# Which engine makes the low parts of the weights, and what the emission plan counts

## Chip, cores and metric

One core of a Trainium2 chip. The metric is the device time of one execution in microseconds. The profile's names of the engines are PE (TensorE's matmuls), PEld (its weight loads), DVE (VectorE), ACT (ScalarE), POOL (GpSimd) and SP (SyncE, which here issues the DMAs).

## What is computed

Two layers of a decoder trunk over 256 tokens of width 1024, all in float32:

```
for l in range(DEPTH):                       # DEPTH = 2
    h = rms_norm(x, attn_norm[l])
    x = x + hybrid_mixer(h, ..., w_in[l], ..., w_out[l])
    h = rms_norm(x, ffn_norm[l])
    x = x + conv_ffn(h, w_up[l], conv_w[l], conv_b[l], w_down[l])
```

`hybrid_mixer` multiplies h with one wide matrix `w_in`, makes three attention branches of the columns (MoBA block attention; NSA with a compressed, a selected and a window part; GLA, a gated linear attention that needs the logarithm of a sigmoid and a cumulative sum), and merges them by gates. `conv_ffn` multiplies with `w_up`, runs a causal convolution of width 3 over one half of the columns, a GELU, a product with the other half, and multiplies with `w_down`.

## The kernel before

**Weights in two parts.** Every weight matrix streams from HBM in blocks of 128 partitions by up to 1024 columns (`raw`, 5 buffers). A block is split into a high part (`whi`, a cast to float32r on ScalarE) and a low part (`wlo` = `raw` - `whi`, a subtraction), 3 buffers each. The activations are split in the same way (`hh`, `hl`; `fh`, `fl` in the feed-forward part). Each product is three matmuls: high by high, high by low, low by high. Chunks of mode A have activations as the stationary operand and up to 512 weight columns moving; chunks of mode B (the up projection and some columns of the input projection) have weights stationary and 256 tokens moving. A block of a mode B chunk is used by 24 matmuls, and a chunk of it has two blocks.

**Who makes the low part.** `Pump.split` emits one ScalarE cast for a block, and then divides the low part's columns between VectorE and GpSimd. The division comes from the plan's times of the two engines: columns go to GpSimd until both would end together. `lo(a, b)` emits VectorE's subtraction, `lo(a, b, G)` GpSimd's. The first two blocks of the kernel are handled apart, in `first`; the second one's low part stands on GpSimd.

**The emission plan.** The program is straight-line code, and each engine runs its instructions in the order in which they were emitted. That order is chosen while the program is built. `Plan` keeps a modelled time for each engine (`t`) and for each piece of a tile (`at`). Every emitted instruction passes through `Eng`, whose line 135 is the line that nearly all rows of the profile carry; `Plan.note` takes its start as the latest of its engine's time, TensorE's time and its inputs' times plus 0.15 us, and adds `Plan.cost`. The main loop (`run_phase`) emits the matmuls of block after block. Everything else (the attention branches, the epilogues) is written as generators; a generator that yields is resumed by `tick` when TensorE's modelled time has passed the modelled end of its last step plus 0.8 us. So a modelled cost sets no time on the chip, but it sets how many matmuls TensorE has in its queue ahead of a small step, and in which order VectorE, ScalarE and GpSimd find their work. `run_phase` holds a block back in the plan until its high part is there, not its low part.

**Places that the text speaks of.** `nsa_keys` normalises keys (`kn`), transposes them on TensorE into PSUM (`pst`) and scales them into `kt` by four VectorE operations, which TensorE then reads for the scores. `compress` copies `kd` for another transposition. `gla_gate` adds a bias, takes Exp and Ln on ScalarE behind a load of their activation table, and on VectorE subtracts (`tt<-tt`) and scans into `b`, which `gla` reads. In the up projection a pair of chunks makes two tiles of columns: `done_a` scales by the norm (`tt<-pd,rsB`), convolves (four `tt<-tt,pt`), applies the GELU on ScalarE and scales again on GpSimd (`tt<-tt,rsB`); `done_g` multiplies with the other half (`tt<-tt,pd`), casts to `fh` on VectorE and makes `fl` on GpSimd. There are 11 pairs in a layer. Tiles `tt` are 9 scratch buffers.

Of the kernel before, what the change touches and what calls it, by code (L numbers as in the profile page):

```python
# [27 lines left out]
def _aps(args, kw):  # L28
    outs, ins = [], []
    for i, a in enumerate(args):  # L30
        if hasattr(a, "tensor"):
            (outs if i == 0 else ins).append(a)
    for k, a in kw.items():
        if hasattr(a, "tensor"):
            (outs if k in ("out", "accum_out") else ins).append(a)
    return outs, ins


def _free(ap):
    n = 1  # L40
    for d in ap.shape[1:]:
        n *= d
    return n
# [4 lines left out]
    return lo, lo + 1 + sum(abs(s) * (n - 1) for s, n in ap.ap[1:])  # L48


class Plan:


    def __init__(self):
        self.t = {"PE": 0.0, "V": 0.0, "A": 0.0, "G": 1.5, "S": 0.6, "D": 0.0}
        self.at = {}
        self.step = 0.0
        self.n = 0
# [14 lines left out]
    def cost(self, e, f, outs, ins, kw):  # L73
        n = max(_free(a) for a in outs[:1] + ins[:1]) if outs else 0
        if e == "PE":
            m = _free(outs[0])
            if f == "transpose":
                return 0.109
            if ins[0].dtype == F32R:
                return max(0.107, m / 2400 + 0.0025)  # L80
            return max(_free(ins[0]) / 600, m / 600 + 0.004)
        if e == "V":
            if f == "reciprocal":
                return 0.07 + n * 0.0084
            if f == "tensor_tensor_scan":
                return 0.07 + n * 0.00104
            if f == "memset":
                return 0.05 + n * 0.0003
            fast = f in ("tensor_scalar", "tensor_copy") and "pst" not in str(ins[0].tensor) and "pd" not in str(ins[0].tensor)
            ptr = len(ins) > {"tensor_scalar": 1, "scalar_tensor_tensor": 2}.get(f, 9)  # L90
            return 0.07 + 0.06 * ptr + n * (0.00052 if fast else 0.00104)
        if e == "S":
            return 0.06
        if e == "A":
            if f == "dma_start":
                return 0.06
            return 0.11 + n * 0.00083 + 0.05 * ("pst" in str(ins[0].tensor) or "pd" in str(ins[0].tensor)) + 0.09 * (len(outs) - 1 + hasattr(kw.get("bias"), "tensor"))
        if f == "dma_start":
            return 1.0
        if f in ("memset", "iota"):  # L100
            return 0.1 + n * 0.0009
        if kw.get("op") == OP.pow:
            return 0.35 + 0.165 * n
        return 0.1 + n * (0.0036 if f == "tensor_copy" else 0.0023)

    def note(self, e, f, args, kw):
        outs, ins = _aps(args, kw)
        if not outs:
            return
        self.n += 1  # L110
        st = max([self.t[e], self.t["PE"]] + [self.get(a) + 0.15 for a in ins])
        if f == "dma_start":
            self.t[e] = st + self.cost(e, f, outs, ins, kw)
            self.t["D"] = max(self.t["D"], self.t[e] + 1.0) + 4 * _free(outs[0]) * outs[0].shape[0] / 360e3
            en = self.t["D"] + 1.5
        else:
            en = st + self.cost(e, f, outs, ins, kw)
            self.t[e] = en
        lat = 0.2 if e == "PE" else 0.0
        for a in outs:  # L120
            self.put(a, en + lat)
        if f != "dma_start":
            self.step = max(self.step, en + lat + 0.15)
# [29 lines left out]
def trunk_kernel(ctx, tc, x, rel_bias, attn_norm, w_in, moba_q_norm, moba_k_norm,  # L153
# [13 lines left out]
    pd = ctx.enter_context(tc.tile_pool(name="pd", bufs=4, space=PSUM))  # L167
# [7 lines left out]
    def take(s, n=1):  # L175
        while True:
            t = s.at(n)
            if t is not None and t <= plan.t["PE"]:
                break
            plan.step = max(plan.step, t or 0.0)  # L180
            yield
        s.take(n)

    def give(s, n=1):
        s.free += [plan.step] * n
# [4 lines left out]
    def pst():  # L190
        return ps.tile([128, 512], F32, name="pst", tag="pst")

    def tt():
        return tp.tile([128, 512], F32, name="tt", tag="tt", bufs=NT)

    plan = Plan()
    V, A, G, PE, SP = (Eng(plan, e, g) for e, g in (("V", nc.vector), ("A", nc.scalar), ("G", nc.gpsimd),
                                                    ("PE", nc.tensor), ("S", nc.sync)))

    def avail(*aps):  # L200
        while max(plan.get(a) for a in aps) > plan.t["PE"]:
            plan.step = max([plan.step] + [plan.get(a) for a in aps])
            yield
# [14 lines left out]
    class Pump:  # L218
# [43 lines left out]
        def split(self):  # L262
            n, hi, lo = self.open()
            hi(0, n)
            w = self.blocks[self.ns - 1][1]
            h = self.hl[self.ns - 1][0]
            t0 = plan.get(h)
            v, g = max(plan.t["V"], t0) + 0.07, max(plan.t["G"], t0) + 0.1 + 0.0
            c = n * w
            m = int((v - g + c * 0.00104) / (0.00104 + 0.0023)) // 64 * 64  # L270
            m = c if m > c - 128 else m if m >= 128 else 0
            if m < c:
                lo(0, c - m)
            if m:
                lo(c - m, c, G)

        def ahead(self, d, s):
            while self.nd < min(len(self.blocks), self.ng + d):
# [65 lines left out]
    def wait(*fl):  # L344
        for f in fl:
            while f not in flags:
                yield
# [290 lines left out]
    def make_layer(l):  # L638
        key = lambda *a: (l,) + a
        st = {}  # L640
        T = {}

        def atl(name, shape, dt=F32, **kw):
            t = at.tile(shape, dt, name=name, tag=name, **kw)
            T[name] = t
            return t
# [9 lines left out]
        def setf(f):  # L656
            flags.add(key(f))
# [22 lines left out]
        def gla_gate():  # L680
            ga = T["ga"]
            yield from avail(ga)
            yield from take(sem_ps)
            p = pst()
            for t in range(2):
                PE.transpose(p[:16, t * 128:t * 128 + 128], ga[:, t], ident)
            yield from take(sem_t)
            gg = tt()
            gw, gl = gg[:16, 0:256], gg[:16, 256:512]
            SP.dma_start(gw, gla_gate_w[l])  # L690
            yield
            V.tensor_copy(gl, p[:16, :256])
            give(sem_ps)
            yield
            yield from wait(("par", l))
            yield from avail(gw)
            yield from take(sem_ps)
            p = pst().rearrange("p (c s) -> p c s", c=2)
            for c in range(2):
                PE.matmul(p[:, c], gw[:, c * 128:c * 128 + 128], gl, start=True, stop=True)  # L700
            give(sem_t)
            yield
            yield from take(sem_t, 2)
            u, m = tt(), tt()
            pt = par[l][0]
            for c in range(2):
                A.activation(u[:, c * 256:c * 256 + 256], p[:, c], AF.Abs, bias=pt[:, 22 + c:23 + c])
                V.tensor_scalar(m[:, c * 256:c * 256 + 256], p[:, c], pt[:, 22 + c:23 + c], 0.0,
                                op0=OP.add, op1=OP.min)
            give(sem_ps)  # L710
            A.preload_act_table_set("natural_log_exp_and_others")
            A.activation(u, u, AF.Exp, scale=-1.0)
            A.activation(u, u, AF.Ln, bias=1.0)
            setf("ln")
            V.tensor_sub(m, m, u)
            b = atl("b", [128, 512])
            V.tensor_tensor_scan(b, smask, m, 0.0, op0=OP.mult, op1=OP.add)
            give(sem_t, 2)
            setf("b")
# [427 lines left out]
        def done_gv(half):  # L1147
            def f(p):
                yield from wait((key("n1"), "rs"))
                gv = grp("gvv", 2048, 1024).rearrange("p (t c) -> p t c", t=2)  # L1150
                T["gvv"] = gv
                if half:
                    ga = atl("ga", [128, 2, 16])
                    for t in range(2):
                        A.activation(ga[:, t], p[t][:, 256:272], AF.Copy, scale=rs(t))
                for t in range(2):
                    A.activation(gv[:, t, half * 256:half * 256 + 256], p[t][:, 0:256], AF.Copy, scale=rs(t))
                give(sem_pd, 2)
                if half:
                    normal.append(gla_gate())  # L1160
                else:
                    setf("gv")
            return f
# [420 lines left out]
    for l, ly in enumerate(layers):  # L1584
        st = ly["st"]
# [64 lines left out]
```

## Time and profile before

| | |
|---|---|
| median of 3 runs | 859.55 us (858.62 to 860.23) |
| the profiled execution, its own time | 859.51 us |
| its span, first to last instruction | 857.7 us |
| instructions | 13958 |
| mean granted TensorE clock | 0.994 |
| DMA | 143.57 MB, mean 167 GB/s |

The span is what the trace shows; about 1.8 us of the execution's own time lie outside it. The layers are alike: the input projection with the attention, the branch and output projections, the up projection (layer 0: from about 244 us; layer 1: from about 662 us) and the down projection.

### The profile page before, as it was taken

Reading aid. Unit: us, or ns where it says so; the run is one execution under the profiler, and the core shown is the slowest. Engines: PE = TensorE matmul, PEld = TensorE weight load, DVE = VectorE, ACT = ScalarE, POOL = GpSimd, SP = SyncE. Lnnn points to the kernel's source line nnn. Section 1 sums busy time; section 2 is a strip of 40 time slices with the busy share of each in tenths; the row PEclk is TensorE's granted clock in tenths of the full one; section 3 lists DMA queues with packets and bytes.
Section 4 is the critical chain, followed back from the end, with each engine's and each line's share of the span. In section 5 each row is a group of like instructions: output and inputs, shape, how many; then the busy total and the mean of one; then the engine's idle time right before and its main releaser. Section 6 shows DMA issues by size and latency. Waiting matters only on the chain.

```text
span 857.7 us, 13958 instructions
## 1 busy us (share of the span) xinstructions
PE 837.8 (98%) x5173; PEld 750.4 (87%) x5173; DVE 576.3 (67%) x880; ACT 431.8 (50%) x666; POOL 470.6 (55%) x341
## 2 busy tenths in 40 slices
PE   7989999999999989999999999999999999999998
PEld 7878888888889989998898898888888999999886
DVE  4665787456757788884446776854595499887642
ACT  5454555554456445453446545464544644454431
POOL 4533654446546665666545347535575476665653
PEclk9998999999999999999999999999999999999999
DMA  6883444445555555556558444445456555556571
GB/s 199 249 255 88 157 121 130 144 128 192 185 162 173 171 174 182 174 167 217 172 174 229 123 146 123 133 130 156 162 182 196 151 159 183 183 163 210 185 218 49
DMA packets 109976, 143.57 MB, mean 167 GB/s; under 512 B 13677, under 2 KB 71380, under 8 KB 109780
## 3 DMA queue, kind: packets, MB, share of 16 engines
q1 hardware_dynamic: 109892, 142.68, 53.7%
q8 instruction: 41, 0.67, 0.3%
q14 instruction: 27, 0.22, 0.1%
q10 hardware_dynamic: 16, 0.00, 0.0%
HBM read 141.60 MB, written 2.63 MB: 168 GB/s over the span
## 4 chain that ended last, share of the span: by engine, by line
PE 80%; DVE 10%; ACT 3%; issue 2%; DMA 2%; POOL 2%; SPq 0%; DVEq 0%; ACTq 0%; POOLq 0%
PE pd L135 70%; PE pst L135 8%; DVE tt L135 5%; DVE wlo L135 4%; DMA raw<-in_w_in_dram 2%; PE po L135 2%; ACT whi L135 1%; ACT tt L135 1%; POOL tt L135 1%; POOL wlo L135 1%; DVE qz L135 1%; POOL mqs L135 0%; DVE kn L135 0%; POOL fl L135 0%; ACT L135 0%
## 5 line engine op out<-in xcount | busy, mean ns | idle before, releaser
L135 POOL TENSOR_TENSOR wlo<-raw,whi 128x256 fp32r<-128x256 f32 (+10 forms) x222 | 317.8, 1435 | 289.2 <-ACT whi L135 275.7
L135 ACT CAST whi<-raw 128x1024 fp32r<-128x1024 f32 (+3 forms) x267 | 271.5, 1021 | 267.2 <-PE pd L135 124.0
L135 DVE TENSOR_TENSOR wlo<-raw,whi 128x768 fp32r<-128x768 f32 (+12 forms) x261 | 268.2, 1035 | 186.7 <-ACT whi L135 183.5
L135 PE MATMUL pd<-hh,wlo 128*128 128x256 f32 x768 | 217.8, 284 | 4.6 <-DVE wlo L135 4.6
L135 PE MATMUL pd<-hh,whi 128*128 128x256 f32 x768 | 218.7, 285 | 0.2
L135 PE MATMUL pd<-hl,whi 128*128 128x256 f32 x768 | 217.5, 283 | 1.1 <-DVE hl L135 1.1
L135 PE MATMUL pd<-whi,hh 128*128 128x512 f32 (+3 forms) x512 | 206.4, 403 | 3.2 <-ACT whi L135 2.2
L135 PE MATMUL pd<-wlo,hh 128*128 128x512 f32 (+3 forms) x512 | 193.6, 378 | 0.2 <-DVE wlo L135 0.2
L135 PE MATMUL pd<-whi,hl 128*128 128x512 f32 (+3 forms) x512 | 193.7, 378 | 0.0
L135 PEld LDWEIGHTS pd<-hh,wlo 128*128 128x128 f32 x768 | 147.3, 192 | 5.6 <-DVE wlo L135 5.6
L135 PEld LDWEIGHTS pd<-hl,whi 128*128 128x128 f32 x768 | 147.3, 192 | 1.8 <-DVE hl L135 1.5
L135 PEld LDWEIGHTS pd<-hh,whi 128*128 128x128 f32 x768 | 147.3, 192 | 0.9 <-ACT hh L135 0.7
L135 PEld LDWEIGHTS pd<-whi,hh 128*128 128x128 f32 x512 | 98.2, 192 | 19.1 <-ACT whi L135 2.4
L135 PEld LDWEIGHTS pd<-whi,hl 128*128 128x128 f32 x512 | 97.8, 191 | 17.4
L135 PEld LDWEIGHTS pd<-wlo,hh 128*128 128x128 f32 x512 | 98.2, 192 | 14.1 <-DVE wlo L135 0.4
L135 DVE SCALAR_TENSOR_TENSOR tt<-tt,pt 128x255 f32<-128x255 f32 x88 | 86.4, 1003 | 1.6
L135 PE MATMUL pd<-whi,fh 128*128 128x512 f32 x176 | 68.7, 390 | 0.0
L135 PE MATMUL pd<-wlo,fh 128*128 128x512 f32 x176 | 68.7, 390 | 0.0
L135 PE MATMUL pd<-whi,fl 128*128 128x512 f32 x176 | 68.5, 389 | 0.0
L135 POOL TENSOR_TENSOR fl<-tt,fh 128x512 fp32r<-128x512 f32 x22 | 41.4, 1882 | 31.3 <-DVE fh L135 31.3
L135 ACT ACTIVATE tt<-tt 128x512 f32<-128x512 f32 (+1 forms) x52 | 26.0, 531 | 32.9 <-DVE tt L135 32.8
L135 ACT ACTIVATE tt<-tt,nm 128x128 f32<-128x128 f32 (+1 forms) x48 | 21.4, 447 | 41.9 <-DVE nm L135 41.9
(210 smaller groups left out, 837.9 us busy)
## 6 DMA issues: line engine op xcount, KB each, us to landing
raw<-in_w_up_dram SPq DMA_DIRECT2D x88, 512.0 KB
raw<-in_w_in_dram SPq DMA_DIRECT2D x84, 512.0 KB
raw<-in_w_down_dram SPq DMA_DIRECT2D x44, 512.0 KB
raw<-in_w_out_dram SPq DMA_DIRECT2D x16, 512.0 KB
raw<-in_w_branch_gla_dram SPq DMA_DIRECT2D x8, 512.0 KB
raw<-in_w_in_dram SPq DMA_DIRECT2D x8, 396.0 KB
raw<-in_w_branch_moba_dram SPq DMA_DIRECT2D x4, 512.0 KB
raw<-in_w_branch_nsa_dram SPq DMA_DIRECT2D x4, 512.0 KB
```

Source lines behind the costliest of these rows:

```text
L135: return g(*args, **kw)
```

## The change

The change edits the plan and its use. In `Plan.cost` it raises prices of matmuls, scans, VectorE operations and accumulating activations. In `Plan.note` it counts 1.3 us for an explicit load of an activation table, and it keeps one time, `port`, for all operations of VectorE and GpSimd that read no PSUM: such an operation is modelled as starting only when the last one of either engine has ended. In `Pump.split` GpSimd gets columns of a low part only when VectorE's modelled time runs past GpSimd's, the port's and the cast's, at least 256 columns; otherwise VectorE makes the whole low part in one instruction. In `gla_gate` a yield stands between the logarithm on ScalarE and VectorE's subtraction and scan.

```diff
+def _psum(ap):
+    return any(n in str(ap.tensor) for n in ("pst", "pd_", "po_"))
...
     def __init__(self):
+        self.port = 0.0
...
             if ins[0].dtype == F32R:
-                return max(0.107, m / 2400 + 0.0025)
-            return max(_free(ins[0]) / 600, m / 600 + 0.004)
+                return max(0.112, m / 2400 + 0.0135)
+            return max(0.112 if _free(ins[0]) < 65 else 0.224, m / 600 + 0.008)
...
             if f == "tensor_tensor_scan":
-                return 0.07 + n * 0.00104
+                return 0.09 + n * 0.0021
...
-            return 0.07 + 0.06 * ptr + n * (0.00052 if fast else 0.00104)
+            return 0.09 + 0.06 * ptr + n * (0.00052 if fast else 0.00109)
...
-            return 0.11 + n * 0.00083 + 0.05 * ("pst" in str(ins[0].tensor) or "pd" in str(ins[0].tensor)) + 0.09 * (len(outs) - 1 + hasattr(kw.get("bias"), "tensor"))
+            return 0.11 + n * 0.00083 + 0.05 * ("pst" in str(ins[0].tensor) or "pd" in str(ins[0].tensor)) + 0.2 * (len(outs) - 1) + 0.09 * hasattr(kw.get("bias"), "tensor")
...
     def note(self, e, f, args, kw):
         outs, ins = _aps(args, kw)
+        if f == "preload_act_table_set":
+            self.t[e] = max(self.t[e], self.t["PE"]) + 1.3
...
         st = max([self.t[e], self.t["PE"]] + [self.get(a) + 0.15 for a in ins])
+        port = e in "VG" and f != "dma_start" and ins and not any(_psum(a) for a in ins)
+        if port:
+            st = max(st, self.port)
...
             self.t[e] = en
+            if port:
+                self.port = en
...
-            t0 = plan.get(h)
-            v, g = max(plan.t["V"], t0) + 0.07, max(plan.t["G"], t0) + 0.1 + 0.0
+            t0 = plan.get(h) + 0.15
             c = n * w
-            m = int((v - g + c * 0.00104) / (0.00104 + 0.0023)) // 64 * 64
-            m = c if m > c - 128 else m if m >= 128 else 0
+            m = int((plan.t["V"] - max(plan.t["G"], plan.port, t0) - 0.1) / 0.0023) // 64 * 64
+            m = min(c, m) if m >= 256 else 0
+            if m:
+                lo(c - m, c, G)
             if m < c:
                 lo(0, c - m)
-            if m:
-                lo(c - m, c, G)
...
             A.activation(u, u, AF.Ln, bias=1.0)
             setf("ln")
+            yield
             V.tensor_sub(m, m, u)
```

## Rows read from the trace of the kernel before

**Rows 1.** The page: busy us (share of the span) and instructions of each engine.
```profile
PE 837.8 (98%) x5173; PEld 750.4 (87%) x5173; DVE 576.3 (67%) x880; ACT 431.8 (50%) x666; POOL 470.6 (55%) x341
```

**Rows 2.** Waits of PE: waiter, releaser, us in total, times, longest.
```profile
PE pd L135 <- DVE wlo L135: 4.8, 6, 2.5
PE pst L135 <- DVE kt L135: 3.0, 1, 3.0
PE pd L135 <- ACT whi L135: 2.2, 1, 2.2
...
PE pst L135 <- DVE kd L135: 0.6, 1, 0.6
```

**Rows 3.** Windows: length, busy us of five engines, PEclk, DMA share, GB/s.
```profile
19.60:22.90 3.30, 3.30 (x12) 3.29 (x12) 3.08 (x9) 0.86 (x1) 3.00 (x4) 0.50 0.63 178
65.20:70.70 5.50, 5.48 (x15) 4.56 (x16) 3.07 (x13) 1.33 (x6) 0.00 (x0) 0.50 0.52 172
303.00:372.00 69.00, 68.39 (x570) 68.39 (x571) 58.77 (x67) 34.86 (x42) 43.56 (x30) 1.00 0.58 183
```

**Rows 4.** Timeline of ACT, layer 0, input projection: start us, us, instruction, count.
```profile
56.88 1.28 ACT L135 ACT_TABLE_LOAD   x1
58.17 1.30 ACT L135 ACTIVATE tt<-tt 128x512 f32<-128x512 f32 x2
```

**Rows 5.** Timeline of DVE there, 59 to 67 us; idle before, releaser in brackets.
```profile
59.50 0.69 DVE L135 TENSOR_TENSOR tt<-tt 128x512 f32<-128x512 f32 x1 [2.12 <-ACT tt L135]
60.23 1.22 DVE L135 TENSOR_TENSOR_SCAN b<-smask,tt 128x512 f32<-128x512 bf16 x1
61.37 3.31 DVE L135 TENSOR_TENSOR wlo<-raw,whi 128x320 fp32r<-128x320 f32 x2
64.60 1.98 DVE L135 TENSOR_SCALAR kt<-pst,pt 64x256 f32<-64x256 f32 x4
```

**Rows 6.** Timeline of POOL in the same stretch.
```profile
60.48 3.38 POOL L135 TENSOR_TENSOR wlo<-raw,whi 128x704 fp32r<-128x704 f32 x2 [7.04 <-ACT whi L135]
```

**Rows 7.** Groups of instructions: count, busy us, mean ns, idle before, releaser.
```profile
L135 POOL TENSOR_TENSOR wlo<-raw,whi 128x256 fp32r<-128x256 f32 (+10 forms) x222 | 317.8, 1435 | 289.2 <-ACT whi L135 275.7
...
L135 DVE TENSOR_TENSOR wlo<-raw,whi 128x768 fp32r<-128x768 f32 x140 | 142.0, 1014 | 164.8 <-ACT whi L135 162.1 <-PE pst L135 2.6
...
L135 DVE SCALAR_TENSOR_TENSOR tt<-tt,pt 128x254 f32<-128x254 f32 x44 | 47.5, 1080 | 1.6
```

**Rows 8.** Timeline of DVE, up projection of layer 0, 298 to 304 us.
```profile
298.78 4.04 DVE L135 SCALAR_TENSOR_TENSOR tt<-tt,pt 128x255 f32<-128x255 f32 x4
302.74 1.61 DVE L135 TENSOR_TENSOR wlo<-raw,whi 128x640 fp32r<-128x640 f32 x2
```

**Rows 9.** Timeline of POOL in the same stretch.
```profile
300.36 2.18 POOL L135 TENSOR_TENSOR wlo<-raw,whi 128x384 fp32r<-128x384 f32 x2
```

**Rows 10.** Timeline of DVE, input projection of layer 1.
```profile
466.71 0.69 DVE L135 TENSOR_TENSOR tt<-tt 128x512 f32<-128x512 f32 x1 [2.12 <-ACT tt L135]
```

**Rows 11.** Timeline of DVE, up projection of layer 0, one operation at 291 us, then one pair.
```profile
291.28 0.48 DVE L135 SCALAR_TENSOR_TENSOR tt<-tt,pt 128x254 f32<-128x254 f32 x1
...
342.18 0.69 DVE L135 TENSOR_TENSOR tt<-tt,pd 128x512 f32<-128x512 f32 x1 [1.88 <-POOL tt L135]
342.91 0.43 DVE L135 CAST fh<-tt 128x512 fp32r<-128x512 f32 x1
343.25 1.22 DVE L135 TENSOR_TENSOR wlo<-raw,whi 128x1024 fp32r<-128x1024 f32 x1
...
350.29 0.68 DVE L135 TENSOR_TENSOR tt<-pd,rsB 128x512 f32<-128x512 f32 x1
...
353.72 0.69 DVE L135 TENSOR_TENSOR tt<-tt,pd 128x512 f32<-128x512 f32 x1 [1.88 <-POOL tt L135]
```

**Rows 12.** Timeline of POOL in that pair.
```profile
340.86 1.29 POOL L135 TENSOR_TENSOR tt<-tt,rsB 128x512 f32<-128x512 f32 x1
```

**Rows 13.** Timeline of POOL: the first reader of `b` in layer 0.
```profile
93.47 1.03 POOL L135 TENSOR_TENSOR tt<-b 128x512 f32<-128x512 f32 x1
```

## Prediction

> **What bounds the kernel now.** I read the busy line of the page first. TensorE is busy 837.8 of 857.7 us, VectorE 576.3, GpSimd 470.6 [rows 1]. No other engine is near the span, so an edit that moves work between VectorE and GpSimd can pay only where TensorE now stands still, or where it runs at half clock. So the second view is TensorE's own waits [rows 2]: six waits for a low part from VectorE, 4.8 us in total with one of 2.5; one of 3.0 for `kt`; 2.2 for a high part from ScalarE; 0.6 for `kd`; the rest is smaller. The third is the granted clock by stretch [rows 3]. Two stretches ran at 0.50, the 1.2 GHz level: 19.6 to 22.9 us, behind the 2.2 us wait, and 65.2 to 70.7 us, behind the 3.0 us wait; TensorE worked through both, so they cost half their length, 1.65 and 2.75 us. Behind the 2.5 us wait the clock stayed at 1.00 (303 to 372 us) [rows 3]. What can be won is therefore 4.8 + 3.0 + 2.2 + 0.6 + 1.65 + 2.75 = 15.0 us, and the question is who makes VectorE late at these places.
>
> **How the two engines share.** At 60.48 us GpSimd takes two low parts that last 3.38 us [rows 6]; VectorE's scan ends at 61.45, and its own two low parts, 320 and 768 columns, then last 3.31 us [rows 5]. A low part of 1024 columns alone takes VectorE 1.22 us [rows 11], so 1088 columns in two instructions should take about 1.4. The missing 1.9 us is the time in which GpSimd worked. The same shows in the groups: a low part on GpSimd takes 1435 ns in the mean, 256 columns most often, where 512 columns on GpSimd alone take 1.29 us [rows 7, 12], so 256 alone would be near 0.65. One engine stands while the other runs when both work on SBUF. An operation of VectorE on PSUM (0.68 and 0.69 us for 512 columns) shows no such stretch [rows 11].
>
> **Low parts on VectorE alone.** GpSimd's share of a full block, given to it at the same time as VectorE's, ends after about 1.4 us [rows 7], its wait included; VectorE alone takes 1.22 [rows 11]. So the low part is complete about 0.2 us earlier, GpSimd loses most of its low parts, and VectorE gains about 256 columns a block (a quarter of 1.22, 0.3 us) but loses the waits for GpSimd. By the new rule GpSimd gets columns only where VectorE's planned queue runs at least 0.69 us past the last planned SBUF operation (0.1 + 256 x 0.0023), that is behind two or more PSUM operations in a row; I expect under 60 low parts on it, and its busy time at some 155 to 210 us: 470.6 less the 317.8 of all 222 low parts, plus at most 60 of about a microsecond [rows 1, 7]. A raw buffer comes free that much earlier too, so SP's next weight load starts no later; the DMA share was 0.58 in the up projection [rows 3].
>
> What does this pay in the up projection? There the stretch 298 to 304 shows it: four `tt<-tt,pt` operations take 4.04 us [rows 8] where one alone takes 0.48 [rows 11], because GpSimd holds 2.18 us of low parts among them [rows 9] and `fl` ahead of those; the next low part starts at 302.74 [rows 8], and TensorE has waited 2.5 us for it. Four at 0.48 would end 2.1 us sooner. Of the 4.8 us in rows 2 I take 4.0 and leave 0.8 for waits that stay; bounds 0 and 4.8. **B = -4.0.**
>
> Is VectorE then fast enough? A pair of chunks is 96 matmuls. Two passes of the same place are 342.18 and 353.72 us, 11.54 us apart [rows 11], 0.120 us a matmul, the new plan's price (the old one was 0.109). VectorE's own work in it: 4 low parts x 1.22 + 0.68 + 4 x 0.48 + 0.69 + 0.43 = 8.60 us; GpSimd's two remaining operations, 2 x 1.29 = 2.58 [rows 11, 12]. If nothing of the two overlapped, 11.18 us: it fits with 0.36 to spare. Before, GpSimd's low parts came on top, and it fitted. Cost 0; without that cover every 0.1 us a pair costs 2.2 us over 22 pairs.
>
> **Plan's prices, table load and the yield.** In layer 0 VectorE stands 2.12 us in front of `tt<-tt` for ScalarE's Exp and Ln [rows 5], behind a table load of 1.28 us [rows 4] that the old plan counts as nothing. Then come a scan of 1.22 us (old price 0.60, new 1.17), and 3.31 us of low parts; only then `kt` at 64.60, and TensorE waits 3.0 us. The edits meet each link: the yield lets other tasks' VectorE work, `kt` too, stand ahead of `tt<-tt` and the scan; the load is counted; the port is counted. Had `kt` (4 in 1.98 us) stood in the hole of 2.12 us, TensorE would not have waited at all; had it only lost GpSimd's 1.9 us, 1.1 us would be left. What the yield makes late is `b`: its first reader starts at 93.47 us [rows 13], 32 us after the scan, so a few us cost nothing; two scratch buffers of nine are held as long. Bounds 0 and 3.0 + 2.75 = 5.75; I take most, since two mechanisms must both fail for the wait to stay whole. **A = -5.0.** In layer 1 the same hole of 2.12 us stands ahead of `kd` [rows 10]; of the 0.6 for `kd` I take 0.5, bounds 0 and 0.6. **C = -0.5.**
>
> A table load: `tt<-tt` on ScalarE starts 1.29 us after the load's start [rows 4], so 1.3 is the price. The Trainium skill, "ScalarE: Activation LUTs", What ACT_TABLE_LOAD costs, counts a drain of about 1.38 us on top, 2.66 us a switch, by which the new price is half of what it should be and the gain 2.7 us smaller over the two layers, near 854.7 (an estimate). The trace does not agree with that drain.
>
> The start is not touched: the 2.2 us wait for ScalarE and the 1.65 us behind it stay, 0. The tail after the last matmul stays, 0.
>
> **What the new order may cost.** Every instruction is placed by the plan, so all of the order moves. A matmul of 256 columns now counts 0.120 instead of 0.109: a delay of 5 us is filled with 42 matmuls and not 46, and the small TensorE steps of the attention stand some 0.5 us earlier per 5 us. VectorE's and ScalarE's prices rise too, which sets them back. New waits the trace cannot show; below, 0 (or a gain: all remaining small waits go, another 1 us); above, one like that for `kt` with its clock, 5.75. I take 2.0, near the 2.2 and 2.5 us waits of rows 2. **E = +2.0.**
>
> Sum: -5.0 - 4.0 - 0.5 + 2.0 = -7.5 us. The profiled execution took 859.51 us (span 857.7 and 1.8 around it), 0.04 from the median of 859.55: **852.0 us**. A measurement of this kernel tells 0.2%, 1.7 us, from no change.
>
> **Rivals.**
> *The wait for `kt` stays.* The plan puts it late again, A = 0: 857.0. For it: the high part that VectorE turns to next comes from the same late ScalarE, whose cast starts only at the end of that table load, Exp and Ln; against it: the 2.12 us hole. 15%.
> *VectorE becomes the bound of the up projection.* If it stands 1.88 us for GpSimd's `tt` as now and the whole 1.29 for `fl`, a pair is 8.60 + 1.88 + 1.29 = 11.77 us against 11.54: 22 x 0.23 = 5.1 us, and B is lost: 852.0 + 4.0 + 5.1 = 861.1, no change that can be told. Against it: `fl` can run beside VectorE's 1.37 us on PSUM, and `tt` mostly has no low part ahead of it any more. 8%.
> *The re-timed order makes new waits (slower).* Place: the input projection of either layer, where `kd`, `kn`, `kt` feed TensorE. The margin that the too fast matmul price gave is gone; if A fails and layer 1 gets a wait of 3.0 us with its 2.75 us of half clock, 852.0 + 5.0 + 5.75 = 862.8. It decides when the new waits, with what A loses, pass 9.5 us in all. For it: the layer 1 hole has the same size and 0.6 us came of it; against: the prices are nearer to the rows at each place I compared. 17%.
> *A table load costs twice its 1.28 us.* VectorE would stand 1.28 us again in each layer: 852.0 + 2.6 = 854.6. Rows 4 speak against it: 2%. The Trainium skill, "ScalarE: Activation LUTs", What ACT_TABLE_LOAD costs, gives about that.
> *All is won and nothing lost:* 859.5 - 5.75 - 4.8 - 0.6 - 1.0 = 847.3, less a few us where the start's wait shortens by chance: 843 to 848, 8%.
> Forecast (848 to 856): 50%.
>
> Range: the forecast with the deep case, both partial ones and the nearer half of the slow one, 845 to 863 us. About 4 in 100 lie below it, 10 above. Faster by over 0.2%: 50 of the forecast, 12 of the 15, 1 of the 8, 1 of the 17, 2 and 8, 0.74. Within 0.2%: 3, 4 and 2 of the three rivals, 0.09. Slower: 3 of the 8 and 14 of the 17, 0.17.
>
> **What would show it.** GpSimd's low parts under 60 and its busy time under 210 us; VectorE's low parts some 315 us in total with the 1024-column ones near 1.22 in the mean; `tt<-tt,pt` well under its mean of 1080 ns [rows 7], near 600; no wait for `wlo` over 1 us in the up projections; clock 1.00 from 62 to 71 us and no wait for `kt` over 1 us; VectorE's 2.12 us hole before `tt<-tt` gone in both layers. Wrong it would be if TensorE's waits in the two input projections sum to more than before, or if the up projection's pairs take over 11.7 us.

## The result, and the profile after

The changed kernel takes **864.87 us** (median of 20 runs, 861.18 to 873.30), the kernel before, measured with it, 859.04 (20 runs, 857.55 to 862.68): a ratio of 1.0087 [1.0065, 1.0109], slower. The forecast was 852.0, and the time lies above its range. The 20 runs fall into two groups of ten, 861.2 to 862.3 us with a mean granted clock of 0.990 to 0.992 and 867.5 to 873.3 with 0.974 to 0.982, and the median lies between them; the profiled execution, 868.38 us with 0.982, is of the second, so stretches of half clock show longer in it than in half of the runs.

The busy line of the page, against [rows 1]: GpSimd lost two thirds of its work, VectorE gained only 12 us.

```profile
PE 845.0 (98%) x5173; PEld 757.6 (87%) x5173; DVE 588.6 (68%) x883; ACT 429.8 (50%) x666; POOL 167.5 (19%) x129
```

The groups of instructions that answer to [rows 7] (count, busy us, mean ns, idle before, releaser):

```profile
L147 DVE TENSOR_TENSOR wlo<-raw,whi 128x1024 fp32r<-128x1024 f32 (+3 forms) x264 | 340.0, 1291 | 202.1 <-ACT whi L147 201.1
L147 DVE SCALAR_TENSOR_TENSOR tt<-tt,pt 128x255 f32<-128x255 f32 x88 | 42.2, 502 | 1.6
L147 POOL TENSOR_TENSOR tt<-tt,rsB 128x512 f32<-128x512 f32 x22 | 40.9, 1859 | 124.0 <-ACT tt L147 124.0
L147 POOL TENSOR_TENSOR wlo<-raw,whi 128x272 fp32r<-128x272 f32 (+4 forms) x10 | 14.2, 1426 | 36.5 <-ACT whi L147 36.5
```

So far it went much as forecast. What didn't is seen in TensorE's waits (waiter, releaser, total us, times, longest), against [rows 2]:

```profile
PE pst L147 <- DVE kn L147: 4.9, 2, 3.2
PE pst L147 <- DVE tt L147: 4.3, 1, 4.3
PE pd L147 <- DVE hl L147: 3.2, 4, 0.9
PE pd L147 <- ACT whi L147: 2.1, 1, 2.1
...
PE pd L147 <- ACT hh L147: 1.0, 1, 1.0
PE pd L147 <- DVE wlo L147: 0.4, 1, 0.4
```

The waits for `wlo` are down from 4.8 us to one of 0.4 at the kernel's start, and the wait for `kt` is gone. In their place TensorE waits 4.9 us for `kn` (once in each layer) and 4.3 for the `tt` of the compress additions, all in the input projections. The windows (length, busy us of five engines, PEclk, DMA share, GB/s) against [rows 3]:

```profile
20.10:23.50 3.40, 3.40 (x13) 3.39 (x12) 3.09 (x15) 0.85 (x1) 0.38 (x1) 0.50 0.52 163
54.20:74.70 20.50, 16.20 (x59) 14.44 (x59) 11.27 (x25) 3.65 (x7) 0.58 (x1) 0.50 0.42 125
303.00:372.00 69.00, 69.00 (x578) 69.00 (x577) 53.26 (x66) 34.24 (x43) 18.57 (x12) 1.00 0.60 183
484.30:491.10 6.80, 6.80 (x27) 6.14 (x26) 3.52 (x9) 0.98 (x2) 0.00 (x0) 0.50 0.27 77
```

The stretch of the up projection that had the 2.5 us wait now begins some 8 us later and runs without one at full clock (the third row: 69.00 of 69.00). But behind the waits of the input projections TensorE works 16.20 and 6.80 us at 1.2 GHz, which costs half of that, 8.1 + 3.4 us; before, one such stretch of 5.5 us cost 2.75 [rows 3].

Who is late shows on VectorE's timeline of layer 0 (start, duration; idle before and releaser in brackets), against [rows 5]:

```profile
48.99 0.42 DVE L147 TENSOR_REDUCE nqs<-tt 128x4 f32<-128x256 f32 x1 [2.81 <-ACT tt L147]
...
50.89 1.23 DVE L147 TENSOR_TENSOR wlo<-raw,whi 128x1024 fp32r<-128x1024 f32 x1 [0.31 <-ACT whi L147]
52.03 0.90 DVE L147 TENSOR_TENSOR kn<-a,kss 128x128 f32<-128x128 f32 x4
52.85 2.48 DVE L147 TENSOR_TENSOR tt<-tt 128x512 f32<-128x512 f32 x1
55.36 1.22 DVE L147 TENSOR_TENSOR_SCAN b<-smask,tt 128x512 f32<-128x512 bf16 x1
56.51 1.20 DVE L147 TENSOR_TENSOR wlo<-raw,whi 128x1024 fp32r<-128x1024 f32 x1
57.62 1.74 DVE L147 TENSOR_TENSOR tt<-pst,pt 64x256 f32<-64x256 f32 x4
```

and on ScalarE's timeline there, against [rows 4]:

```profile
45.28 1.28 ACT L147 ACT_TABLE_LOAD   x1
46.58 1.29 ACT L147 ACTIVATE tt<-tt 128x512 f32<-128x512 f32 x2
47.78 0.82 ACT L147 ACTIVATE mv<-pd,rs 128x256 f32<-128x256 f32 x2
48.49 0.47 ACT L147 ACTIVATE tt<-pd,rs 128x256 f32<-128x256 f32 x1
```

GpSimd's timeline there, against [rows 6]:

```profile
52.82 1.96 POOL L147 TENSOR_TENSOR wlo<-raw,whi 128x832 fp32r<-128x832 f32 x1 [0.24 <-ACT whi L147]
```

TensorE's, with its two waits:

```profile
52.67 0.86 PE L147 MATMUL pst<-ident,kn 128*128 128x128 f32 x4 [1.72 <-DVE kn L147]
...
58.53 3.62 PE L147 MATMUL pst<-tt,w 128*128 128x30 f32 x16 [4.30 <-DVE tt L147]
```

The gate's table load now stands at 45.28 us (56.88 before, [rows 4]), ahead of the squares of the NSA queries (`tt<-pd,rs`, 48.49). Before, the squares came first, on ScalarE's timeline:

```profile
42.81 0.47 ACT L135 ACTIVATE tt<-pd,rs 128x256 f32<-128x256 f32 x1
```

VectorE still stands idle for ScalarE, 2.81 us, but now it waits for those squares, and all that is behind them is late: TensorE waits 1.72 us for `kn`. Subtraction and scan, which before stood in that hole [rows 5], come at 52.85, between `kn` and the compress additions. GpSimd took an 832-column low part 0.03 us earlier, and the subtraction lasts 2.48 us instead of 0.69 [rows 5]; with the scan and a low part the additions start at 57.62, and TensorE has waited 4.30 us. VectorE's timeline in layer 1, against [rows 10]:

```profile
472.43 1.22 DVE L147 TENSOR_TENSOR wlo<-raw,whi 128x1024 fp32r<-128x1024 f32 x1 [3.06 <-ACT whi L147]
...
477.01 0.69 DVE L147 TENSOR_TENSOR tt<-tt 128x512 f32<-128x512 f32 x1
477.73 1.22 DVE L147 TENSOR_TENSOR_SCAN b<-smask,tt 128x512 f32<-128x512 bf16 x1
478.87 1.20 DVE L147 TENSOR_TENSOR wlo<-raw,whi 128x1024 fp32r<-128x1024 f32 x1
479.99 2.63 DVE L147 TENSOR_TENSOR kn<-a,kss 128x128 f32<-128x128 f32 x4
```

GpSimd's beside it:

```profile
479.54 2.33 POOL L147 TENSOR_TENSOR wlo<-raw,whi 128x832 fp32r<-128x832 f32 x1 [1.78 <-ACT whi L147]
```

Here the hole of 2.12 us [rows 10] has become one of 3.06, ended by the high part that ScalarE casts behind Exp and Ln; subtraction and scan stand right ahead of `kn`, and beside GpSimd's low part `kn` lasts 2.63 us. TensorE's wait for `kn` there is 3.17 us, the rest of the 4.9. The sign that was asked for, clock 1.00 from 62 to 71 us, is not there (0.50), and neither hole is gone. The sign of being wrong came: the waits in the two input projections are 9.2 us for `kn` and `tt`, against 3.6 for `kt` and `kd` before [rows 2].

The Trainium skill, "SBUF — State Buffer", Who interferes with whom, says that a VectorE instruction with two inputs in SBUF and a GpSimd one that reads SBUF exclude each other, and that the later one stands until the earlier has ended. Both places agree within 0.14 us: 54.78 us (GpSimd's end) plus 0.69 is 55.47, where the subtraction ends at 55.33; in layer 1 481.87 plus 0.89, the time of the four `kn` operations in run 2, is 482.76, where they end at 482.62.

### The profile page after: what moved, and what is told of

Its sections match the earlier page's. It is cut to its first block, busy times and chain, and to the rows that moved or that the text cites. A ratio compares the mean times of both kernels' runs of the same rounds, so it can differ in the third digit from the quotient of the medians.

```text
span 866.6 us, 13437 instructions
## 1 busy us (share of the span) xinstructions
PE 845.0 (98%) x5173; PEld 757.6 (87%) x5173; DVE 588.6 (68%) x883; ACT 429.8 (50%) x666; POOL 167.5 (19%) x129
## 3 DMA queue, kind: packets, MB, share of 16 engines
HBM read 141.60 MB, written 2.63 MB: 166 GB/s over the span
## 4 chain that ended last, share of the span: by engine, by line
PE 90%; DVE 4%; ACT 2%; issue 1%; SPq 1%; DMA 0%; DVEq 0%
PE pd L147 79%; PE pst L147 9%; DVE wlo L147 2%; PE po L147 2%; ACT whi L147 1%; SPq L147 1%; DVE tt L147 1%; DMA w<-in_cmp_k_w_dram 0%; DVE hl L147 0%; DVE kn L147 0%; DVE xs L147 0%; ACT L147 0%; ACT tt L147 0%; ACT hh L147 0%; DVE grp L147 0%
## 5 line engine op out<-in xcount | busy, mean ns | idle before, releaser
L147 DVE TENSOR_TENSOR wlo<-raw,whi 128x1024 fp32r<-128x1024 f32 (+3 forms) x264 | 340.0, 1291 | 202.1 <-ACT whi L147 201.1
L147 POOL TENSOR_TENSOR tt<-tt,rsB 128x512 f32<-128x512 f32 x22 | 40.9, 1859 | 124.0 <-ACT tt L147 124.0
L147 DVE SCALAR_TENSOR_TENSOR tt<-tt,pt 128x255 f32<-128x255 f32 x88 | 42.2, 502 | 1.6
L147 POOL TENSOR_TENSOR fl<-tt,fh 128x512 fp32r<-128x512 f32 x22 | 31.1, 1414 | 58.9 <-DVE fh L147 58.9
L147 PEld LDWEIGHTS pd<-whi,fl 128*128 128x128 f32 x176 | 33.0, 188 | 6.9
```

The source lines that it names most:

```text
L147: return g(*args, **kw)
```

## The experiments

Three theories stood after the result. **Y**: the yield does the harm, since it takes subtraction and scan out of the hole. **G**: GpSimd's 832-column low parts do, since they hold VectorE. **P**: the new prices do, since they bring the gate ahead of the query chain. Ratios are to the kernel before, measured beside each run (its medians there 859.0 to 859.7); differences from the changed kernel are from its median of 864.87.

**Run 1**, the changed kernel without the yield.

```diff
             setf("ln")
-            yield
             V.tensor_sub(m, m, u)
```

> The changed kernel with the yield alone taken out. Theory Y (the yield moved the subtraction and the scan out of a hole, in which VectorE stood anyway, to a place right ahead of the operations that TensorE waits for): TensorE's three long waits in the two input projections (1.7, 4.3 and 3.2 us, 9.2 in all) fall under 4 us, and the time under 857 us. Theory G (GpSimd's two low parts of 832 columns hold VectorE at those places) and theory P (the new prices bring the gate's work ahead of the NSA queries' work): the waits stay over 7 us and the time stays above 861.

856.30 us, 0.9963 [0.995, 0.9977], 8.6 below the changed kernel. Behind the start, no wait in either input projection is over 1.12 us. Y is supported; whether the yield harms alone or only with the rest is open. Without it the order of VectorE and ScalarE changes from the gate of layer 0 on, so this run doesn't say yet which instruction's place it is.

**Run 2**, the changed kernel with no low part on GpSimd but those of the start.

```diff
-            m = min(c, m) if m >= 256 else 0
+            m = 0
```

> The changed kernel with no low part on GpSimd at all outside the start. Theory G: the waits of 9.2 us in the input projections fall by 3 to 4 us, since VectorE gains about 1.0 us of work but loses 1.8 us of standing at each of two places and the waits end the half clock sooner; 858 to 861 us. Theories Y and P: at most 2 us of the waits go, the time is within 2 us of the changed kernel's 862 or 872.

859.54 us, 1.002 [0.9994, 1.0045], 5.3 below. VectorE's timeline at the same two places:

```profile
52.33 0.68 DVE L147 TENSOR_TENSOR tt<-tt 128x512 f32<-128x512 f32 x1
...
473.01 0.89 DVE L147 TENSOR_TENSOR kn<-a,kss 128x128 f32<-128x128 f32 x4
```

The subtraction is 1.80 us shorter and `kn` 1.74; TensorE's waits there fall by 1.81 (4.30 to 2.49) and 1.74 (3.17 to 1.43). G is a part of the cause, not the whole.

**Run 3**, the new split and the port alone: old prices, no counted table load, no yield. Against the changed kernel:

```diff
-                return max(0.112, m / 2400 + 0.0135)
+                return max(0.107, m / 2400 + 0.0025)
...
-                return 0.09 + n * 0.0021
+                return 0.07 + n * 0.00104
...
-            self.t[e] = max(self.t[e], self.t["PE"]) + 1.3
...
-            yield
```

> The kernel before with the new division of low parts and the port in the plan alone: old prices, table load not counted, no yield. Theories Y and P: no wait of over 3 us in the input projections, the waits for low parts in the up projections (4.5 us) gone: 850 to 856 us. Theory G: GpSimd's few large low parts hold VectorE in the input projections here too, waits there over 5 us, time 857 to 863.

853.84 us, 0.9941 [0.992, 0.9962]. The waits for low parts are 0.6 us in all; the largest wait left is one of 3.41 at 53.24, over the 3 us that Y and P allowed, for products that stand behind subtraction and scan (`tt<-pd,nqs` at 52.69). The new split and the port pay by themselves.

**Run 4**, prices and counted table load alone: old split, no port, no yield. Against the changed kernel:

```diff
-            st = max(st, self.port)
...
-            m = min(c, m) if m >= 256 else 0
+            m = c if m > c - 128 else m if m >= 128 else 0
...
-            yield
```

> The kernel before with the new prices and the counted table load alone: old division of low parts, no port, no yield. Theory P: the gate's table load comes ahead of the NSA queries' squares in layer 0 and long waits of over 6 us appear in the input projections: 863 us or more. Theories Y and G: no new wait of over 3 us there; the waits of the up projections stay: 857 to 862 us.

862.49 us, 1.0026 [1.0008, 1.0045]. A wait of 3.2 us for `kn` stands in layer 1 here too, behind two low parts and beside a 768-column one of GpSimd. What P named did not come: in layer 0 the table load still stands behind the squares, and no wait there is over 1.34 us behind the start.

```profile
42.91 0.47 ACT L143 ACTIVATE tt<-pd,rs 128x256 f32<-128x256 f32 x1
...
50.48 1.28 ACT L143 ACT_TABLE_LOAD   x1
```

So these prices do a little harm without the yield, but with the old split they don't bring the gate ahead.

**Run 5**, the kernel before with the yield alone.

```diff
             setf("ln")
+            yield
             V.tensor_sub(m, m, u)
```

> The kernel before with only the yield added (old prices, old split, no port, no counted table load). Theory Y, the yield by itself does harm, since it takes the subtraction and the scan out of the place where VectorE waits for ScalarE anyway: about 9 us slower than the kernel before, near 868, because taking it out of the changed kernel was worth 8.6 us. Theory P, the yield only does harm where the new prices have brought the gate ahead of the NSA query chain: in layer 0 little changes (a low part takes the place of the wait, the wait for kt stays between 1 and 4 us), in layer 1 the subtraction and scan move from the 2.12 us hole to the place ahead of kn and add up to 1.9 us and some half clock there; 858 to 863.

866.87 us, 1.0093 [1.0077, 1.0108]: as much as the whole loss, from one line. VectorE's timeline in layer 0:

```profile
60.30 0.96 DVE L135 TENSOR_TENSOR wlo<-raw,whi 128x768 fp32r<-128x768 f32 x1 [3.06 <-ACT whi L135]
61.18 1.23 DVE L135 TENSOR_TENSOR tt<-tt 128x512 f32<-128x512 f32 x1
62.44 1.90 DVE L135 TENSOR_TENSOR_SCAN b<-smask,tt 128x512 f32<-128x512 bf16 x1
```

Two rows of TensorE's waits:

```profile
PE pst L135 <- DVE kn L135: 3.6, 2, 1.8
PE pst L135 <- DVE kt L135: 3.5, 1, 3.5
```

The window behind the waits for `kn`:

```profile
478.50:488.70 10.20, 9.75 (x38) 8.78 (x38) 5.92 (x15) 0.69 (x1) 0.04 (x1) 0.50 0.36 103
```

In layer 0 no ready work came into the hole. The next instruction in VectorE's order was a low part, whose high part ScalarE casts only after the table load, Exp and Ln: the hole grew from 2.12 to 3.06 us, and `kt`, still behind subtraction and scan, is later than before (3.5 against 3.0). In layer 1 they stand ahead of `kn`: 3.6 us and a stretch of half clock of 10.2 us. So P in this form, by which the yield costs little on the old prices, falls.

**Run 6**, the changed kernel with subtraction and scan 12 us later: `hold(12)` resumes the gate when TensorE's modelled time has moved on by 12 us.

```diff
             setf("ln")
-            yield
+            yield from hold(12)
             V.tensor_sub(m, m, u)
```

> The changed kernel with a delay of 12 us of planned time in the place of the bare yield, so that subtraction and scan are issued behind kn, the compress additions and grp in both layers, behind kt in layer 0; the gate's table load, Exp and Ln stay where the change puts them. Theory Y, it is the place of subtraction and scan that makes TensorE wait: the waits for kn in layer 1 and for the compress addition go, 9.2 us of waits fall to under 4, time 854 to 858, as without the yield. Theory P, it is the early gate, whose table load, Exp and Ln hold ScalarE ahead of the query squares: the waits go down by the 1.9 us of subtraction and scan a layer only, and the half clock behind them stays; 860 to 863. Theory G, GpSimd's 832-column low parts stretch whatever stands beside them: the waits fall by half, 858 to 861.

**849.71 us**, 0.9915 [0.9885, 0.9944], 15.2 below the changed kernel, under what any of the three theories said, and the lowest median of all. VectorE's timeline, two rows of layer 0 and two of layer 1:

```profile
54.42 1.74 DVE L147 TENSOR_TENSOR tt<-pst,pt 64x256 f32<-64x256 f32 x4
...
59.74 0.69 DVE L147 TENSOR_TENSOR tt<-tt 128x512 f32<-128x512 f32 x1
...
470.25 0.90 DVE L147 TENSOR_TENSOR kn<-a,kss 128x128 f32<-128x128 f32 x4
...
474.54 0.68 DVE L147 TENSOR_TENSOR tt<-tt 128x512 f32<-128x512 f32 x1
```

The two waits in question:

```profile
PE pst L147 <- DVE kn L147: 1.7, 1, 1.7
...
PE pst L147 <- DVE tt L147: 0.7, 1, 0.7
```

The early gate, its table load (45.72 us) and GpSimd's two low parts of 832 columns (53.26 and 471.64) are still there; what differs is the place of two instructions. Taken from the two traces, the orders of TensorE, VectorE, ScalarE and GpSimd are the same in all else, so this run shows the cause with the least beside it. The wait for `kn` in layer 1 is gone, that for the additions fell from 4.30 to 0.65, and the 1.7 for `kn` in layer 0, which comes of the early gate, stayed.

**Run 7**, run 3 with the yield.

```diff
             setf("ln")
+            yield
```

> The new split and the port with the old prices, as in the third run, and the yield added to it. In the third run TensorE waited 3.41 us at 53.2 us for the products that stand behind subtraction and scan; here these products and grp stand ahead of them in layer 0, kn too. Theory Y, the yield does harm wherever it is: 860 or more. Theory P, the yield does harm only with the new prices: the 3.41 us wait and the 1.7 us of half clock behind it go, less 1 us for subtraction and scan ahead of the compress additions; 849 to 854, not slower than the third run's 853.8.

855.90 us, 0.9964 [0.995, 0.9978], between what Y and P said. The 3.41 us wait went, as the order said, but three waits of 3.4 us together (1.72, 0.99 and 0.68, for `pT`, `om` and `hh`) came at 192 to 195, at the end of the attention, and one of 1.16 for `grp` in layer 1. Not told apart from run 3: in this order the yield did no harm that can be told, nor did it pay. Why the waits at 192 to 195 came stays open.

**Run 8**, the changed kernel with the old prices of VectorE and ScalarE; matmul prices, table load, split, port and yield stay.

```diff
-                return 0.09 + n * 0.0021
+                return 0.07 + n * 0.00104
...
-            return 0.09 + 0.06 * ptr + n * (0.00052 if fast else 0.00109)
+            return 0.07 + 0.06 * ptr + n * (0.00052 if fast else 0.00104)
...
```

> The changed kernel with the old prices for VectorE and ScalarE alone (matmul prices, counted table load, split, port and yield stay). The order of emission then puts the params copy and the gate of layer 0 behind the query chain again, as before the change. Theory P by these two engines' prices: the waits for kn at 52.7 and for the compress addition at 58.5 go, those in layer 1 stay about as they are (the order there has the same subtraction, scan and low part ahead of kn); 10 to 12 us of waits and half clock in layer 0 fall to 3 or 4, time 856 to 859. Theory Y: the yield stays and so does the loss, 863 to 866.

852.58 us, 0.9927 [0.9911, 0.9943], 12.3 below the changed kernel and lower than either theory said. In layer 0 no wait over 0.44 us is left between 20 and 75 us, and one of 1.50 for `pT` stands at 75.95; in layer 1 the wait for `kn` stays, 3.04:

```profile
PE pst L147 <- DVE kn L147: 3.0, 1, 3.0
...
PE pst L147 <- DVE kt L147: 0.4, 1, 0.4
```

The table load of layer 0 is back at 55.05 us, behind the squares (42.19). So those two engines' prices set the gate of layer 0 in front of the query chain, but only with the new split and port: run 4 has the prices without them, and there it stayed behind. The yield has no part in that: in run 1, without it, the table load stands at 44.88 us, ahead of the squares (48.09).

**Run 9**, run 6 with no low part on GpSimd but those of the start.

```diff
-            m = min(c, m) if m >= 256 else 0
+            m = 0
```

> The sixth run (subtraction and scan 12 us later), with no low part on GpSimd besides those of the start. Theory G, GpSimd's 832-column low parts hold VectorE wherever they stand: the 1.74 us wait for kn and the half clock behind it shrink again as they did between the changed kernel and the second run (5 us there), 844 to 847. Theory Y, they only cost where kn and the compress additions stand right behind the subtraction and the scan: no change, 848 to 851.

853.87 us, 0.9938 [0.9911, 0.9964] (850.12 to 858.12, run 6 848.36 to 856.91): not told apart from run 6, not lower, and above what both theories said. The wait for `kn` in layer 0 stays, 1.75, so G's share of it isn't there. GpSimd's low parts cost 5.3 us in the changed kernel's order (run 2), where TensorE waits for the VectorE operations beside them, and nothing that can be told in this one.

**Run 10**, the kernel before with the delay of 12 us.

```diff
             setf("ln")
+            yield from hold(12)
             V.tensor_sub(m, m, u)
```

> The kernel before, with only a delay of 12 us of planned time ahead of subtraction and scan (old prices, old split, no port). Place theory: they then stand behind kt in both layers, so the wait for kt of 3.0 us and its 2.75 us of half clock fall by the 3.1 us that subtraction and scan lasted there, no wait for kn of over 1 us comes in layer 1, and the waits for low parts in the up projections stay at some 4.8 us: 852 to 855, 12 to 15 us below the run with the bare yield. Rival, any move out of the 2.12 us hole costs, since a low part takes its place: 860 or more.

857.65 us, 0.998 [0.9967, 0.9993]: 9.2 below run 5, but above the 852 to 855 that the place alone should give. The wait for `kt` fell to 1.22 and no wait for `kn` is over 0.2; 4.8 us for low parts stayed, and the wait for ScalarE at the start was 3.3 instead of 2.2.

**Run 11**, run 8 with the delay of 12 us in place of the yield.

```diff
-            yield
+            yield from hold(12)
```

> The eighth run (the changed kernel with the old prices of VectorE and ScalarE) with the delay of 12 us in the place of the bare yield. Place theory: its wait for kn of 3.04 us in layer 1 and the half clock behind it go, since subtraction and scan stand behind the query products there: 847 to 850. If the wait stays, kn is late for the low parts ahead of it and not for subtraction and scan: 851 to 853.

852.42 us, 0.9901 [0.9872, 0.9931]. The 3.04 us for `kn` in layer 1 went, as the place theory has it, and 2.7 us of other waits (2.01 for `pT` and two for `tt`, at 75 to 78 us) with a stretch of half clock came, where run 8 had 1.50 for `pT`. The median is not told apart from run 8's.

**Run 12**, run 3 with the delay of 12 us.

```diff
             setf("ln")
+            yield from hold(12)
```

> The third run (new split and port, old prices) with the delay of 12 us. Place theory: the 3.41 us wait behind subtraction and scan goes, with the 1.7 us of half clock: 848 to 851, which would make the new split with the delay as good as the sixth run and the new prices worth nothing by themselves. If the new prices are worth something, it stays 2 us or more above the sixth run's 849.7.

852.65 us, 0.992 [0.9905, 0.9935]. The 3.41 us wait went and the 3.4 us at 192 to 195 came, as in run 7. It isn't told apart from run 6 (0.9885 to 0.9944), so whether the new prices are worth anything beside the right place stays open.

## Why the prediction was wrong, point by point

**B held.** Waits for low parts in the up projections: 4.0 of 4.8 us forecast, all won, though they were 4.5; the rest of the 4.8 stood at the kernel's start, where 0.4 stands now. GpSimd made 10 low parts (under 60 forecast) and was busy 167.5 us (155 to 210); VectorE's low parts took 340.0 us (315) at 1291 ns in the mean, the four convolution steps 502 ns each (near 600). VectorE didn't become the bound. Run 3, with the new split and the port alone, is 5.6 us below the kernel before beside it, but its order differs in other places too. And the new split has a price that no term had: TensorE waits 1.9 to 3.2 us for `hl` in all its runs, 1.0 to 1.1 with the old split (runs 4, 5 and 10, and before):

```profile
PE pd L135 <- DVE hl L135: 1.1, 2, 0.6
```

**A reading that its rows don't show**, in "How the two engines share". GpSimd stood still beside all but 0.1 us of the operations on PSUM in [rows 11], so their 0.68 and 0.69 us say nothing on stretching. Another place before the change does, a VectorE operation of the same kind inside one of GpSimd's (two timelines):

```profile
264.05 0.68 DVE L135 TENSOR_TENSOR tt<-pd,rsB 128x512 f32<-128x512 f32 x1
...
263.21 1.51 POOL L135 TENSOR_TENSOR wlo<-raw,whi 128x256 fp32r<-128x256 f32 x1 [1.59 <-ACT whi L135]
```

It took 0.68 us there too, so the reading was right.

**A failed at one sentence**, that with the yield "other tasks' VectorE work, `kt` too," would stand in the hole and TensorE "would not have waited at all". The order is fixed while the program is built, and next in it behind the yield was a low part that needs the same ScalarE. The rival for `kt` had named just this, at 15%. Run 5 shows the yield alone: where A had -5.0 us for it, the load and the port, it gave +7.9. That a few us of delay for `b` cost nothing fits run 6, which delays it further; the cost was not in who waits for the scan, but in what the scan was put in front of. The wait for `kt` did go in the changed kernel, where the whole gate stands earlier; in run 8, where layer 0's gate stands late again, it is 0.44 us.

**C** had the sign right for `kd` (its 0.6 us went), and the layer paid 3.17 for `kn`.

**E was the term mis-sized: +2.0**, where its own upper bound, 5.75, was too low as well: in the profiled execution the new waits of 9.2 us and the 11.5 us of half clock behind them make 20.7. The rival that came true, new waits in the input projection, had 17%; its place was right, its time of 862.8 near the 864.87 by luck, since it took the wait for `kt` as kept and one new wait in layer 1, where that wait went and three others came; its mechanism held only in part, if at all. It named the matmul price, but run 8 keeps that price and has no such wait in layer 0: there the prices of VectorE and ScalarE, with the new split (run 8 against run 4), and the yield (runs 1, 5, 6) made the waits. In layer 1 it stays open. Run 7 differs from run 8 by the old matmul prices and the uncounted table load, and has no wait for `kn` there where run 8 has 3.04, so one of these two has a part; no run takes them one by one.

The 9.2 us of new waits in the input projections, taken away in the order changed kernel, run 2, run 6, divide so: 1.7 for `kn` in layer 0 from the early gate (still there in runs 2 and 6, gone in run 8, where the gate is late); 1.81 + 1.74 from GpSimd's 832 columns (run 2 less the changed kernel); 1.84 + 1.43 from subtraction and scan standing in front (run 6 less run 2); 0.65 left. The shares overlap: the move alone (run 6 less the changed kernel), with GpSimd's parts in place, takes 3.65 + 3.17 = 6.8. Half clock behind them costs 11.5 us where it had cost 2.75 [rows 3].

**The sum in the profiled executions.** TensorE's waits, all rows of the view added, went from 15.7 to 17.5 us: +1.8, with the 4.4 won on low parts in it, and with 2.1 more for `hl` (3.2 against 1.1), which no term had. Half clock went from 1.65 + 2.75 to 1.7 + 8.1 + 3.4: +8.8. Together +10.6 against a measured 868.38 - 859.51 = 8.9; the 1.7 us between are not accounted for.

**The table load** was priced right: Exp starts 1.30 us after it.

## What to carry to other kernels

When a fixed order lets work pass an idle engine, look at the very next instruction in that engine's order and at whether its inputs come from the engine that is being waited for; if they do, the hole stays and the work that filled it is now in someone's way. Price a moved instruction by what it is put in front of, not by who reads its result: the same two instructions, 1.9 us of VectorE in each layer, were worth 15 us by their place (run 6). And a wait of TensorE is to be priced with the half clock behind it, which here cost more than the waits (11.5 against 9.2 us).

## What the runs showed of the hardware

How long TensorE stays at 1.2 GHz behind a wait varied more than the waits: 20.5 us counted from the start of the 4.30 us wait, though TensorE was busy for all of the 16.2 behind it; 10.2 us behind two of 1.83 and 1.76 (run 5); none behind 2.5 us in the up projection [rows 2, 3]. Nor was it the same each time for one kernel: that of run 6 took from 848.4 us, with a mean granted clock of 1.000, to 856.9, with 0.986.
